# Gated DeltaNet stage: TensorE's order from a planner with four chains and a filler, instead of from the scheduler

## The chip, the cores and the metric

The kernel runs on one core of one Trainium2 chip. The metric is the device time of one execution in microseconds (us), as a median over runs. A core has five engines that work in parallel, each in the order of its own instruction stream: TensorE (PE; its weight loads are listed as PEld), VectorE (DVE), ScalarE (ACT), GpSimd (POOL) and SyncE (SP, which issues DMAs). An instruction that waits for another engine holds everything behind it on its own engine.

## The reference

Two DeepNorm layers over 512 positions of 1024 channels. Each layer is a token mixer, a LayerNorm, a squared-ReLU MLP and a LayerNorm. The mixer of the first layer, where the change lies, is a bidirectional gated DeltaNet with 8 heads of 128 key and 128 value channels:

```python
proj = jnp.matmul(h, w_in)
qkv = silu(_depthwise_conv(proj[..., :A_CONV_CH], conv_w))      # 5 taps, centred
z = proj[..., A_CONV_CH:A_CONV_CH + A_VW]
q = _l2norm(heads(q)) * (A_DK ** -0.5);  k = _l2norm(heads(k))
# per direction, in chunks: (I + A) sol = rhs, A strictly lower triangular; then
v_new = u_c - w_c @ state
o     = qd_c @ state + qk_c @ v_new
state = state * gl_c + kd_c.T @ v_new
o = _rmsnorm(o_f + o_b, norm_g) * silu(z);  out = o @ w_out
```

The second mixer (GLA) and the two MLPs are not touched.

## The kernel before

The function `gdn` keeps x transposed on chip (`xth`, `xtl`: a high and a low part) and treats the 8 heads as objects of `GdnHead`. The work of a head has five parts:

- **project**: four projections of the head, k, q, v and z (PSUM tiles `pjk`, `pjq`, `pjv`, `pjz`), 24 matmuls each: eight k-tiles by the three products of the helper `mm3` (L109, L110, L111). The weights come by DMA to `wst`, ACT casts the high part `wh` (L90) and DVE subtracts the low part `wl` (L91). k, q and v go through the 5-tap convolution `conv`: one multiply on ACT (L1032) and four scalar_tensor_tensor on DVE (L1036) into the tile `sil` of the head (four slots: k, q, v, z); z is copied (L1059). Then ACT loads the Silu table, applies Silu to the whole tile (L1065) and loads the exp/ln table back (L50).
- **rows**: four transposes of k, then four of q (L1082, PSUM tile `ktp`); for k a copy `kt` (L1085); for each four ACT squares with a sum (L1087). A chain of small DVE and ACT operations makes the normalisers and decays, which are split into three bf16 parts (`rsp`, 6 columns), transposed (L1112, `rtp`, 6 rows) and copied to `rt` (L1114).
- **solve**: inverts the triangular systems of both directions, 8 tiles of 128x128 at a time: kk, `ep` (L1147, `sel` times `rt`, a product over 6 rows), exponentials `E`, `ath`, three steps `hp` in blocks of 4, then five levels (4 to 64), each a `lv` product, a DVE or ACT step and two more `lv` products (L1220), then one correction (`nw`), `qk`, and the transposed v (`vt`).
- **recur**: four steps over the chunks, both directions side by side. Each step is a chain: product m1 on PE (L1312), `r` on DVE (L1314), product m2 (L1320), `vd` and `vn` on ACT (L1324, L1326), product m3 (L1332), `sn` on DVE or ACT (L1337, L1335), and again m1. Then 14 products make the output `op` (L1345).
- **finish**: RMSNorm of `op`, four transposes `otp` (L1368), times silu(z), split to `oh` and `ol` for the output projection.

After the heads, `out_pieces` makes the output projection of heads 0 to 5 (PSUM `oa`), and `out_last` adds x and heads 6 and 7 (`ob`), with LayerNorm and transposes.

The program order is a loop over heads: recur of head i-2, solve of i-1, project and rows of i, finish of i-2. The order on each engine is made by the framework's scheduler, which takes the earliest in program order that its own timing model has ready. The parts are generators that yield pairs of numbers, but the loop's `run` throws them away. The tile `sil` has three buffers: the project part of head h waits until head h-3 has let go of its tile. PSUM has three banks for projections, two for the solve (`ac`), two for recur and finish (`ch`) and **one** (`tp`) for kk, ktp, rtp and vt.

Of the kernel before, what the change touches and what calls it, by code (L numbers as in the profile page):

```python
# [17 lines left out]
P = 128  # L18
S = 512
D = 1024  # L20
KT = D // P
NT = S // P
# [779 lines left out]
A_H = 8  # L802
NEG = -1e30


class GdnConst:
# [36 lines left out]
    def masks(self):  # L843
        c, pool = self.c, self.pool
        G = c.nc.gpsimd
# [5 lines left out]
        sf = pool.tile([6, 2, P], F32, name="self", tag="E", bufs=2)  # L851
# [37 lines left out]
        n = P // 4  # L889
# [75 lines left out]
def gdn(c, w_in, conv_w, a_log, dt_bias, norm_g, w_out, ln_g, ln_b, x):  # L965
    tc, nc = c.tc, c.nc
    with c.banks(ch=2, pj=3, tp=1, ac=2), tc.tile_pool(name="gdn", bufs=1) as pool:
        last = load_x(c, x, ("ac", "ch", "tp"))
        g = GdnConst(c, pool, w_in, a_log, dt_bias, conv_w, norm_g, last)
        hi = [c.big.tile([P, 2, S], F32R, name=f"oh{t}", tag=f"xt{t}") for t in range(NT)]  # L970
        lo = [pool.tile([P, S], F32R, name="ol", tag="ol", bufs=A_H) for h in range(A_H)]
        heads = [GdnHead(c, pool, g, h, w_in, hi[h // 2][:, h % 2, :], lo[h]) for h in range(A_H)]
        lhs = lambda k, sl: (hi[k // 2][:, k % 2, sl], lo[k][:, sl])
        z = [[None, None] for t in range(NT)]
        early = list(range(6))

# [6 lines left out]
        def run(*gens):  # L983
            for gen in gens:
                for _ in gen:
                    pass

        done = set()
        for i in range(A_H + 2):
            old, mid, new = (heads[j] if 0 <= j < A_H else None for j in (i - 2, i - 1, i))  # L990
            if old:
                run(old.recur(done))
            if mid:
                run(mid.solve(done))
            if new:
                run(new.project(done), new.rows(done))
            if i >= A_H:
                load_z(i - A_H)
                run(c.out_pieces(w_out, early, lhs, z, "pj", (i - A_H,), 1))
            if old:  # L1000
                run(old.finish(done))
        par = c.load_ln(ln_g, ln_b, lambda j: pool.tile([P, S], F32, name="lnp", tag=("ath", "atl", "a4", "Xd")[j]))
        c.new_x()
        c.new_xt()
        c.out_last(w_out, [6, 7], lhs, z, ("ac", "pj"), par)


class GdnHead:
# [30 lines left out]
    def project(self, done):  # L1039

        c, pool, g, h = self.c, self.pool, self.g, self.h
        A = c.nc.scalar
        sil = pool.tile([P, 4, S], F32, name="sil", tag="sil", bufs=3)
        self.kq = kq = sil[:, 0:2, :]
        self.v, self.sz = sil[:, 2, :], sil[:, 3, :]
        for i, ci in enumerate((A_H + h, h, 2 * A_H + h, 3 * A_H + h)):
            if h == 0 and i == 0:
                ps = g.k0
            else:
                wh, wl = c.wcols(self.w_in, ci * P)  # L1050
                ps = c.bank([P, S], F32, name="pj" + "kqvz"[i], tag="pj")
                for k in range(KT):
                    c.mm3(ps, wh[:, k, :], wl[:, k, :], c.xth[:, k, :], c.xtl[:, k, :], k == 0, k == KT - 1)
                    if k < KT - 1:
                        yield 0.69, 0.0
            if i < 3:
                self.conv(sil[:, i, :], ps, ci)
            else:
                A.copy(self.sz, ps)  # L1059
            if i == 1 and h == 0:  # L1060
                c.exp_ln_after(A.activation(kq, kq, AF.Silu))
                done.add(("kq", h))
            elif i == 3:
                v = sil[:, 2 if h == 0 else 0:4, :]
                c.exp_ln_after(A.activation(v, v, AF.Silu))  # L1065
                done.add(("kq", h))
                done.add(("vz", h))
            yield 0.69, 0.0

    def rows(self, done):  # L1070
# [4 lines left out]
        yield 0.0, 6.0  # L1075
        kq = self.kq
        ssp = c.small.tile([P, 2, NT], F32, name="ssp", tag="ssp")
        junk = pool.tile([P, P], F32, name="junk", tag="junk", bufs=2)
        for i in range(2):
            ps = self.bank("ktp", tag="tp")  # L1080
            for n in range(NT):
                T.transpose(ps[:, n, :], kq[:, i, n * P:(n + 1) * P], c.ident)  # L1082
            if i == 0:
                self.kt = self.t2("kt", 3)
                A.copy(self.kt, ps)  # L1085
            for n in range(NT):
                A.activation(junk, ps[:, n, :], AF.Square, accum_out=ssp[:, i, n:n + 1])  # L1087
            yield 0.45, 4.0 if i == 0 else 6.5
# [14 lines left out]
        rs = c.small.tile([P, NT, 6], BF16, name="rsp", tag="rsp")  # L1103
# [7 lines left out]
        for n in range(NT):  # L1111
            T.transpose(rtp[:6, n, :], rs[:, n, :], g.idb)  # L1112
        self.rt = pool.tile([6, S], BF16, name="rt", tag="rt", bufs=2)
        A.copy(self.rt, rtp[:6, :, :].rearrange("p n i -> p (n i)"))  # L1114
# [13 lines left out]
        self.neg, self.kds = neg, kds  # L1128
        done.add(("rows", h))
        yield 0.25, 1.0  # L1130

    def solve(self, done):
# [9 lines left out]
        yield 0.9, 0.3  # L1142
# [10 lines left out]
        yield 0.63, 1.4  # L1153
# [18 lines left out]
        yield 0.45, 6.0  # L1172
# [3 lines left out]
        for it in range(3):  # L1176
# [6 lines left out]
            if it < 2:  # L1183
                yield 0.25, 0.7
# [4 lines left out]
        yield 0.25, 1.6  # L1189
# [35 lines left out]
        for s in (4, 8, 16, 32):  # L1225
# [10 lines left out]
            yield 0.7 if s == 4 else 0.25, 1.2  # L1236
# [4 lines left out]
            yield 0.5, 1.2  # L1241
# [5 lines left out]
        yield 0.25, 1.2  # L1247
# [6 lines left out]
        yield 0.5, 1.3  # L1254
# [13 lines left out]
        for n in range(NT):  # L1268
            T.matmul(qk[:, n, :], self.kc(n), self.qc(n), start=True, stop=True)
        if h:  # L1270
            yield 0.9, 0.0
            yield "op", h - 1
# [14 lines left out]
        yield "vz", h  # L1287
# [4 lines left out]
        A.copy(self.vt, ps)  # L1292
        done.add(("solve", h))
        yield 0.45, 1.0

    def recur(self, done):
# [4 lines left out]
        yield 0.0, 1.0  # L1301
        states, vns = [{}, {}], [{}, {}]
        cur = [None, None]
        for step in range(NT):
# [10 lines left out]
            if step:  # L1315
                yield 0.45, 0.6
# [11 lines left out]
            yield 0.45, 1.0  # L1328
            if step < NT - 1:
# [9 lines left out]
                yield 0.45, 0.6  # L1339
        self.op = op = self.bank("op", tag="ch")  # L1340
        for n in (1, 2, 0, 3):
# [4 lines left out]
            if n == 2:  # L1346
                yield 1.8, 0.0
        done.add(("op", h))

    def finish(self, done):  # L1350

        c, pool, g, op = self.c, self.pool, self.g, self.op
# [12 lines left out]
        yield 1.6, 6.0  # L1365
# [6 lines left out]
        V.tensor_tensor(self.olo, p, self.ohi.bitcast(F32), ALU.subtract)  # L1372
        done.add(("finish", self.h))
        yield 0.45, 0.0
# [39 lines left out]
```

## Time and profile before

| | |
|---|---|
| median of 3 runs | 1403.77 us (1403.65 to 1403.82) |
| span of the profiled execution | 1401.7 us (2.1 us less than the median) |
| Gated DeltaNet stage in that span | from 0 to about 437 us |
| PE busy | 1366.0 us, 97% of the span |
| DVE, ACT busy | 929.5 us (66%), 689.5 us (49%) |
| granted TensorE clock | 0.998 |

The page gives the busy time of each engine, the span in 40 slices, the chain that ended last and the costliest groups of instructions by line. A group's row has its count, its busy time and the mean duration of one. In the timeline each row has its start, its duration and its count. Matmuls overlap in their pipeline, so that their durations add up to more than the time they occupy; the distance between two starts tells what one occupies.

### The profile page before, as it was taken

The numbers are of one execution on the slowest core, as the hardware profiler recorded it, in microseconds if no ns is written. First come the engines' busy times: TensorE is split into PE (matmuls) and PEld (weight loads), VectorE is DVE, ScalarE is ACT, GpSimd is POOL, SyncE is SP. The second block draws the span as 40 slices with busy tenths as digits, with TensorE's granted clock in tenths as the row PEclk, the third lists the DMA queues.
The fourth block names the chain that finished last, engine by engine and source line by source line (L and its number), as shares of the span: only waits on it lengthen the run. The fifth ranks groups of instructions, "written<-read, shape, count | busy, mean of one in ns | idle before, by whom it ended". The sixth has DMA issues, their size and how long they took to land.

```text
span 1401.7 us, 20232 instructions
## 1 busy us (share of the span) xinstructions
PE 1366.0 (97%) x7933; PEld 1116.8 (80%) x7933; DVE 929.5 (66%) x1541; ACT 689.5 (49%) x1320; POOL 121.3 (9%) x168
## 2 busy tenths in 40 slices
PE   7999999999999999999999999999999999999997
PEld 6777777777777888888887888888878888888886
DVE  5787787778667365655556577877764655656655
ACT  3776657666633454444543354554433644445430
POOL 5000000000003300100000100000002000001000
PEclk9999999999999999999999999999999999999999
DMA  6212111211133964655431222222217666656121
GB/s 171 76 48 59 46 46 46 61 46 46 47 111 96 291 154 148 144 155 120 105 96 44 85 86 73 61 61 61 89 47 225 178 183 150 165 120 134 48 83 52
DMA packets 153030, 142.23 MB, mean 101 GB/s; under 512 B 8399, under 2 KB 123207, under 8 KB 152935
## 3 DMA queue, kind: packets, MB, share of 16 engines
q1 hardware_dynamic: 144112, 111.49, 26.5%
q0 software_dynamic: 8256, 29.37, 10.8%
q8 instruction: 62, 1.02, 0.3%
q14 instruction: 33, 0.27, 0.1%
q10 hardware_dynamic: 567, 0.08, 0.0%
HBM read 113.66 MB, written 2.10 MB: 83 GB/s over the span
## 4 chain that ended last, share of the span: by engine, by line
PE 59%; issue 23%; DMA 6%; ACT 6%; POOL 3%; DVE 2%; SPq 1%; DVEq 0%; POOLq 0%; ACTq 0%
DMA w2r<-w2r 4%; PE pj L109 3%; PE pj L111 3%; PE pj L110 3%; PE pjv L109 3%; PE pjv L111 3%; PE pjv L110 3%; PE scp L688 2%; DMA w2r<-in_mlp_w 2%; PE op L1345 2%; PE pjq L110 1%; PE pjq L111 1%; PE pjq L109 1%; PE op L776 1%; PE lv L1220 1%
## 5 line engine op out<-in xcount | busy, mean ns | idle before, releaser
L91 DVE TENSOR_TENSOR wl<-wst,wh 128x1024 fp32r<-128x1024 f32 x137 | 168.5, 1230 | 194.0 <-ACT wh L90 193.3
L90 ACT CAST wh<-wst 128x1024 fp32r<-128x1024 f32 x137 | 144.0, 1051 | 282.7 <-PE pj L110 170.2
L109 PE MATMUL pj<-xth,wh 128*128 128x512 f32 (+1 forms) x544 | 202.0, 372 | 1.7 <-ACT h L276 0.9
L111 PE MATMUL pj<-xth,wl 128*128 128x512 f32 (+1 forms) x544 | 201.7, 371 | 0.4 <-DVE wl L91 0.4
L110 PE MATMUL pj<-xtl,wh 128*128 128x512 f32 (+1 forms) x544 | 201.6, 371 | 0.4 <-DVE xtl L150 0.3
L91 DVE TENSOR_TENSOR w2l<-w2r,w2h 128x1024 fp32r<-128x1024 f32 x84 | 102.6, 1221 | 68.3 <-ACT w2h L90 68.3
L109 PEld LDWEIGHTS pj<-xth,wh 128*128 128x128 f32 x544 | 102.2, 188 | 20.4 <-ACT h L276 2.3
L110 PEld LDWEIGHTS pj<-xtl,wh 128*128 128x128 f32 x544 | 102.5, 188 | 18.6 <-DVE xtl L150 0.8
L111 PEld LDWEIGHTS pj<-xth,wl 128*128 128x128 f32 x544 | 102.4, 188 | 18.6 <-DVE wl L91 0.8
L90 ACT CAST w2h<-w2r 128x1024 fp32r<-128x1024 f32 x84 | 88.2, 1050 | 57.2 <-DMA w2r<-in_mlp_w 25.5
L303 POOL DMA_DIRECT2D w2r<-w2r x48 | 41.5, 902 | 398.2 <-DVE w2l L91 230.1
L90 ACT CAST ah<-h 128x1024 fp32r<-128x1024 f32 x40 | 42.1, 1054 | 42.1 <-PE pX L110 16.8
L110 PE MATMUL pX<-w2l,ah 128*128 128x512 f32 x144 | 56.1, 390 | 0.0
L109 PE MATMUL pX<-w2h,ah 128*128 128x512 f32 x144 | 56.1, 390 | 0.0
L111 PE MATMUL pX<-w2h,al 128*128 128x512 f32 x144 | 56.1, 390 | 0.0
L109 PE MATMUL pjv<-wh,xth 128*128 128x512 f32 x128 | 54.9, 429 | 0.0
L91 DVE TENSOR_TENSOR al<-h,ah 128x1024 fp32r<-128x1024 f32 x40 | 48.9, 1222 | 5.3 <-ACT ah L90 3.7
L160 ACT ACTIVATE rsy<-rsv 128x1 f32<-128x1 f32 (+1 forms) x28 | 5.6, 201 | 90.9 <-DVE rsv L159 90.9
L111 PE MATMUL pjv<-wh,xtl 128*128 128x512 f32 x128 | 50.2, 392 | 0.0
L110 PE MATMUL pjv<-wl,xth 128*128 128x512 f32 x128 | 49.9, 390 | 0.0
L1168 POOL TENSOR_TENSOR atl<-on,ath 128x512 f16<-128x512 f32 x16 | 20.9, 1306 | 323.4 <-ACT ath L1167 171.5
L109 PE MATMUL pjk<-xth,wh 128*128 128x512 f32 (+1 forms) x112 | 42.1, 376 | 0.5 <-ACT wh L90 0.5
(439 smaller groups left out, 3443.3 us busy)
## 6 DMA issues: line engine op xcount, KB each, us to landing
wst<-in_mlp_w SPq DMA_DIRECT2D x80, 512.0 KB, 4.0
w2r<-in_mlp_w SPq DMA_DIRECT2D x48, 512.0 KB, 4.3
w2r<-w2r POOLq DMA_DIRECT2D x48, 512.0 KB, 5.6
wst<-in_a_w_in SPq DMA_DIRECT2D x32, 512.0 KB, 4.0
wst<-in_b_w_in SPq DMA_DIRECT2D x32, 256.0 KB, 3.0
wst<-in_a_w_out SPq DMA_DIRECT2D x8, 512.0 KB, 3.8
wst<-in_b_w_in SPq DMA_DIRECT2D x8, 512.0 KB, 3.7
wst<-in_b_w_out SPq DMA_DIRECT2D x8, 512.0 KB, 3.6
```

The lines of the kernel that those rows point to most:

```text
L90: nc.scalar.copy(hi, src)
L91: nc.vector.tensor_tensor(lo, src, hi.bitcast(F32), ALU.subtract)
L109: mm(ps, ah, bh, start=start, stop=False, **kw)
L110: mm(ps, ah, bl, start=False, stop=False, **kw)
L111: mm(ps, al, bh, start=False, stop=stop, **kw)
L160: nc.scalar.activation(y, v, AF.Ln)
L303: nc.gpsimd.dma_start(blocks[a + (q,)], blocks[b + (q,)], accum_op=ALU.add)
L688: T.matmul(ps[:, n, :], kh[:, sl], qh[:, sl], start=True, stop=True)
L776: T.matmul(ops, l, r, start=i == 0, stop=i == len(mm) - 1)
L1168: G.tensor_tensor(atl[:, us, :], at, ath[:, us, :], ALU.subtract)
L1220: T.matmul(ps[:, u, :, :], lhs[:, u, :], cols(rhs, u, s, i), start=True, stop=True)
L1345: T.matmul(op[:, n, :], l, r, start=i == 0, stop=i == len(mm) - 1)
```

## The change

A class `Weave` decides the order on PE before the program is built. It walks over five generators: solve, recur, rows and finish, each over all heads one after the other, are the chains, in this order of preference; project, with the output projection of heads 0 to 5 behind it, is the filler. A generator yields either a pair (PE time of what it has just issued, time until its next step is ready) or the name of a mark that must have been set. At each turn the first chain that is ready by the planner's clock issues a step; if none is, the filler issues one (three matmuls, 0.69); if the filler is blocked too, the planner's clock moves on. `in_order` then ties PE's matmuls to that order. The orders of DVE, ACT and SP stay with the scheduler. The waiting times in the yields are new numbers. Head h may start its projections when `op` of head h-3 is issued, and finish of h-4.

z of a head is projected together with the next head: the order is z(h-1), k(h), q(h), v(h), and z(h-1) lies in the tile `sil` of head h. The last z stands alone. The tiles of the 6-row products (`sel`, `rsp`, `rt`) have 128 rows or columns, with zeros in the rest.

```diff
+class Weave:
+    def step(self, name, gen):
+        want = self.wants.get(name)
+        if want is not None and want not in self.done:
+            return "blocked"
+        self.wants[name] = None
+        if self.ready.get(name, 0.0) > self.t:
+            return "late"
+        got = next(gen, None)
+        if got is None:
+            return "over"
+        if isinstance(got[0], str):
+            self.wants[name] = got
+        else:
+            self.t += got[0]
+            self.ready[name] = self.t + got[1]
+        return "ran"
+    def run(self, chains, filler):
+        chains = dict(chains)
+        while chains or filler is not None:
+            for name in list(chains):
+                got = self.step(name, chains[name])
+                if got == "over":
+                    del chains[name]
+                if got in ("ran", "over"):
+                    break
+            else:
+                if filler is not None:
+                    got = self.step("filler", filler)
+                    if got == "over":
+                        filler = None
+                    if got in ("ran", "over"):
+                        continue
+                late = [self.ready[n] for n in chains if self.wants.get(n) is None and self.ready.get(n, 0.0) > self.t]
...
+                if late:
+                    self.t = min(late)
...
-        self.sel = pool.tile([6, 2, P], BF16, name="sel", bufs=1)
+        self.sel = pool.tile([P, 2, P], BF16, name="sel", bufs=1)
+        self.rs = pool.tile([P, NT, P], BF16, name="rsp", bufs=1)
+        G.memset(self.rs, 0.0)
...
-        for i in range(A_H + 2):
-            old, mid, new = (heads[j] if 0 <= j < A_H else None for j in (i - 2, i - 1, i))
-            if old:
-                run(old.recur(done))
-            if mid:
-                run(mid.solve(done))
-            if new:
-                run(new.project(done), new.rows(done))
-            if i >= A_H:
-                load_z(i - A_H)
-                run(c.out_pieces(w_out, early, lhs, z, "pj", (i - A_H,), 1))
-            if old:
-                run(old.finish(done))
+        def project():
+            todo = [(h, ci) for h in range(A_H) for ci in heads[h].weights()] + [(A_H, 4 * A_H - 1)]
...
+                if h < A_H and (i == 0 or todo[i - 1][0] != h):
+                    if h >= 3:
+                        yield "op", h - 3
+                    if h >= 4:
+                        yield "finish", h - 4
+                    heads[h].slots()
...
+                        if k < KT - 1:
+                            yield 0.69, 0.0
...
+                    elif kind == 2:
+                        t = head.sil if h else head.v
+                        if h:
+                            heads[h - 1].sz = head.sil[:, 3, :]
+                        c.exp_ln_after(A.activation(t, t, AF.Silu))
+                        done.add(("kq", h))
...
+            yield "finish", early[-1]
+            for hf in range(2):
+                yield "op", early[-1] + hf
+                load_z(hf)
+                yield from c.out_pieces(w_out, early, lhs, z, "pj", (hf,), 1)
...
+        def each(what):
+            for head in heads:
+                yield from getattr(head, what)(done)
+        with c.in_order(mybir.EngineType.PE):
+            Weave(done).run({w: each(w) for w in ("solve", "recur", "rows", "finish")}, project())
...
+    def weights(self):
+        out = [] if h == 0 else [3 * A_H + h - 1]
+        return out + [A_H + h, h, 2 * A_H + h]
...
         yield "kq", h
-        yield 0.0, 6.0
+        yield 0.0, 4.0 if h == 0 else 5.5
...
-            T.transpose(rtp[:6, n, :], rs[:, n, :], g.idb)
-        self.rt = pool.tile([6, S], BF16, name="rt", tag="rt", bufs=2)
+            T.transpose(rtp[:, n, :], rs[:, n, :], g.idb)
+        self.rt = pool.tile([P, S], BF16, name="rt", tag="rt", bufs=2)
...
-            yield 0.5, 1.2
+            yield 0.5, 1.4
...
-                yield 0.45, 0.6
+                yield 0.45, 1.3
```

In the changed kernel the transposes of rows stand at L1154, the convolution at L1123 and L1127, Silu at L1071, m1, m2, m3 at L1382, L1390, L1402, `op` at L1415 and `otp` at L1439.

**PE, between the last projection before Silu and the transposes of rows, in the middle heads.** The tiles m_… are the PSUM tiles of recur. Before, that last projection is pjz:

```order
L111 MATMUL pjz<-xth,wl 128x512
L109 MATMUL pjk<-xth,wh 128x512
L110 MATMUL pjk<-xtl,wh 128x512
L111 MATMUL pjk<-xth,wl 128x512
L1220 LDWEIGHTS ath
...
L110 MATMUL pjk<-xtl,wh 128x512
L1082 MATMUL ktp<-ident,sil 128x128
```

Between pjz and ktp stand 14 projection matmuls of the next head (pjk) and 24 `lv` products. With the change the last projection is pjv:

```order
L111 MATMUL pjv<-xth,wl 128x512
L1382 MATMUL m_2521<-sn,sil 128x128
L1382 MATMUL m_2525<-sn,sil 128x128
L1390 MATMUL m_2535<-r,xf 128x128
L1390 MATMUL m_2541<-r,xf 128x128
L1402 MATMUL m_2547<-vd,kt 128x128
L1402 MATMUL m_2551<-vd,kt 128x128
L1382 MATMUL m_2555<-sn,sil 128x128
L1382 MATMUL m_2559<-sn,sil 128x128
L1251 LDWEIGHTS a_2498
...
L1154 MATMUL ktp<-ident,sil 128x128 x4
```

Between pjv and ktp now stand eight products of recur and eight `hp` products, and no projection; the next projection matmul on PE comes only behind the 14 `op` products and `rtp`.

**ACT at the same place.** Before:

```order
L90 CAST wh<-wst 128x1024
L1059 COPY sil<-pjz 128x512
L1065 ACT_TABLE_LOAD
L1065 ACTIVATE sil<-sil 128x2048
L50 ACT_TABLE_LOAD
```

With the change:

```order
L1239 CAST ath<-on 128x512
L1123 ACTIVATE sil<-pjv,cw 128x512
L1394 ACTIVATE vd<-m_2535,kds 128x128
L1396 COPY vn<-m_2535 128x128
L1394 ACTIVATE vd<-m_2541,kds 128x128
L1396 COPY vn<-m_2541 128x128
L90 CAST wh<-wst 128x1024
L1071 ACT_TABLE_LOAD
L1071 ACTIVATE sil<-sil 128x2048
L50 ACT_TABLE_LOAD
L1157 COPY kt<-ktp 128x512
L1159 ACTIVATE junk,ssp<-ktp 128x128
```

What Silu waits for was a copy of pjz; it is now the whole convolution of pjv, which begins with the ACTIVATE of L1123 and goes on with four DVE instructions.

**PE at the end of the stage, from the last products of head 7 to its transposes.** Before:

```order
L1345 MATMUL op<-sn,qd 128x128
L109 MATMUL oa<-wh,oh_412 128x512
L110 MATMUL oa<-wl,oh_412 128x512
L111 MATMUL oa<-wh,ol 128x512
...
L1368 MATMUL otp<-ident,fo 128x128 x4
```

With the change:

```order
L1415 MATMUL op<-vn,qke 128x128 x2
L1415 MATMUL op<-sn,qd 128x128
L1439 MATMUL otp<-ident,fo 128x128 x4
L109 MATMUL ob<-wh,oh_416 128x512
L110 MATMUL ob<-wl,oh_416 128x512
```

The 12 `oa` and 11 `ob` matmuls that stood between `op` and `otp` have moved ahead of `op`.

More of the change, by code (lines that the diff above doesn't have):

```diff
@@ L1037, in conv, with slots @@
                                    ALU.mult, ALU.add)
[L1039 to L1068, printed above, removed]
+    def weights(self):
+        h = self.h
+        out = [] if h == 0 else [3 * A_H + h - 1]
+        return out + [A_H + h, h, 2 * A_H + h]
+    def slots(self):
+        self.sil = self.pool.tile([P, 4, S], F32, name="sil", tag="sil", bufs=3)
+        self.kq = self.sil[:, 0:2, :]
+        self.v = self.sil[:, 2, :]
     def rows(self, done):
@@ L1101, in rows @@
         V.tensor_tensor(rw, gc, rk, ALU.add)
-        rs = c.small.tile([P, NT, 6], BF16, name="rsp", tag="rsp")
+        rs = g.rs
         r1 = c.small.tile([P, NT, 2], F32, name="r1", tag="r1")
@@ L1111, in rows @@
         for n in range(NT):
-            T.transpose(rtp[:6, n, :], rs[:, n, :], g.idb)
-        self.rt = pool.tile([6, S], BF16, name="rt", tag="rt", bufs=2)
-        A.copy(self.rt, rtp[:6, :, :].rearrange("p n i -> p (n i)"))
+            T.transpose(rtp[:, n, :], rs[:, n, :], g.idb)
+        self.rt = pool.tile([P, S], BF16, name="rt", tag="rt", bufs=2)
+        A.copy(self.rt, rtp.rearrange("p n i -> p (n i)"))
         V.tensor_tensor(c0, rk, gc, ALU.subtract)
@@ L1364, in finish @@
         V.tensor_tensor(on, op, rs_.unsqueeze(2).to_broadcast([P, NT, P]), ALU.mult)
-        yield 1.6, 6.0
+        yield "vz", self.h
+        yield 0.0, 6.5
         otp = self.bank("otp", tag="ch")
```

75 lines of the change are left out of this document (51 added, 24 removed).

## The prediction

> **What bounds the kernel now.** I read the page's engine totals first, then PE's waits in the stage that changes, then PE's timeline, because the first two cannot both be taken at their word.
>
> ```profile
> PE 1366.0 (97%) x7933; PEld 1116.8 (80%) x7933; DVE 929.5 (66%) x1541; ACT 689.5 (49%) x1320; POOL 121.3 (9%) x168
> PE m L1320 <- DVE r L1314: 1.5, 3, 1.0
> PE hp L1179 <- DVE a L1171: 1.4, 3, 0.8
> 200.00:250.00 50.00, 49.31 (x415) 38.88 (x414) 40.02 (x86) 31.38 (x87) 2.32 (x2) 1.00 0.18 44
> 550.00:600.00 50.00, 50.00 (x221) 41.18 (x220) 30.32 (x31) 23.11 (x27) 6.88 (x8) 1.00 0.66 148
> ```
>
> PE looks full, and the two longest waits in the middle of the stage (60 to 440 us) come to 2.9 us in all. In the window rows (PE, PEld, DVE, ACT, POOL, clock, DMA) the DeltaNet stage has PE at 49.3 of 50 us, DVE at 40.0, ACT at 31.4; the MLP behind it has PE at 50.0. The Trainium skill, Perfetto Trace Analysis (Identifying the Most-Contended Engine), says that matmul busy time does not tell how near PE is to its limit and that the busy share of weight loads does. By that rule 38.9 against the MLP's 41.2 leaves some 5% of the stage to be won, which the trace's starts, below, bear out in kind.
>
> ```profile
> 210.91 0.39 PE L109 MATMUL pjk<-xth,wh 128*128 128x512 f32 x1
> 211.13 0.39 PE L110 MATMUL pjk<-xtl,wh 128*128 128x512 f32 x1
> 211.36 0.39 PE L111 MATMUL pjk<-xth,wl 128*128 128x512 f32 x1
> 211.59 0.41 PE L1220 MATMUL lv<-pz,Xd 128*128 128x64 f16 x8
> 211.83 0.40 PE L1220 MATMUL lv<-Xd,pz 128*128 128x64 f16 x8
> 212.06 0.47 PE L109 MATMUL pjk<-xth,wh 128*128 128x512 f32 x1
> 212.38 0.40 PE L110 MATMUL pjk<-xtl,wh 128*128 128x512 f32 x1
> 212.72 0.33 PE L1082 MATMUL ktp<-ident,sil 128*128 128x128 f32 x1
> 195.90 0.61 PE L1345 MATMUL op<-vn,qke 128*128 128x128 f32 x4
> 196.34 0.61 PE L1345 MATMUL op<-sn,qd 128*128 128x128 f32 x4
> 165.03 1.92 ACT L1065 ACTIVATE sil<-sil 128x2048 f32<-128x2048 f32 x1
> 301.44 1.92 ACT L1065 ACTIVATE sil<-sil 128x2048 f32<-128x2048 f32 x1
> ```
>
> A projection matmul shows 0.39 us but the next starts 0.23 us later; eight `lv` products take 0.24 us, four fp32 products of 128 columns 0.44 us. After a change from small products back to a projection, the first matmul takes 0.32 us, 0.085 more. The Silu of a head comes every 45.5 us (three heads in 136.4 us).
>
> What is PE's own part of that? A head has 96 projection matmuls (96 x 0.228 = 21.9), 100 fp32 products of 128 columns (100 x 0.111 = 11.1), 120 `lv` (3.6) and, counted at 0.03 to 0.23 us each, some 3.4 us of hp, nw, xp, ep and rtp: **40.0 us**. In the order before, a middle head has 26 runs of projections, 26 x 0.085 = **2.2 us**. The rest of the 45.5 us, **3.3 us**, are waits. So the whole that a better order can win is 5.5 us per head.
>
> **The change part by part.**
>
> *Fewer runs.* In the new order a middle head has 12 runs: 1.0 us, a gain of 1.2 us per head.
>
> *Waits.* A head now costs 40.0 + 1.0 + W; it breaks even at W = 4.5. W is not spread any more. The new order puts nine projection matmuls (2.0 us) between most links of solve; at this rate the filler runs ahead to its limit of three `sil` tiles and is then blocked until `op` of an older head. From pjv of a head to `rtp` PE has no projection left: a stretch of 10.2 us of matmul time (15.1 us once, at the third head) in which recur, hp and rows have only each other. In it stands ktp, 2.0 us of PE time behind pjv (eight products of two 0.111 us passes, and hp). What must happen in these 2.0 us:
>
> ```profile
> 200.47 0.39 PE L111 MATMUL pjv<-xth,wl 128*128 128x512 f32 x1
> 201.62 0.68 ACT L1032 ACTIVATE sil<-pjv,cw 128x512 f32<-128x512 f32 x1
> 202.90 0.74 DVE L1036 SCALAR_TENSOR_TENSOR sil<-pjv,cw,sil 128x510 f32<-128x510 f32 x1
> 207.26 0.74 DVE L1036 SCALAR_TENSOR_TENSOR sil<-pjv,cw,sil 128x510 f32<-128x510 f32 x1
> 208.86 0.58 ACT L1059 COPY sil<-pjz 128x512 f32<-128x512 f32 x1
> 209.46 1.28 ACT L1065 ACT_TABLE_LOAD   x1
> 210.75 1.92 ACT L1065 ACTIVATE sil<-sil 128x2048 f32<-128x2048 f32 x1
> 212.69 1.28 ACT L50 ACT_TABLE_LOAD   x1
> 215.08 0.59 ACT L1085 COPY kt<-ktp 128x512 f32<-128x512 f32 x1
> 215.56 0.28 ACT L1087 ACTIVATE junk<-ktp 128x128 f32<-128x128 f32 x1
> ```
>
> With empty queues: 0.7 + 4 x 0.74 + 1.92 = 5.6 us, and 0.2 to hand over, 5.8. In this trace the convolution of pjv ran from 200.7 to 208.0, 7.3 us, because other DVE work stood between its four instructions; with Silu 9.2. Here z's move counts: before, Silu waited for a copy of pjz, 0.58 us, and had 14 projection matmuls to hide in; now it waits for pjv's convolution and has none. So PE, in order, stands still at ktp for 3.8 us (empty queues) to 7.2 us. Behind ktp in PE's order wait m2, hp, m3 and all of solve. Then the one `tp` bank: the second ktp waits for the table load (1.28), the copy (0.5 to its successor) and four squares (0.25 each by their starts), 2.8 us, with `vd` and `vn` of recur now in between (0.8 more); 1.7 us of matmuls stand there, so 1.1 to 1.9 more. Last, `sn` stands on ACT behind eight `E` and one `ath`, and `Xd` behind the second four squares: about 1 us each. What W holds: from 3.8 (Silu alone, with the rest hidden in it) to 7.2 + 1.9 + 1 = 10.1. I take **9.0**, near the upper end, since the trace's convolution had the long latency. Then a middle head takes 50.0 us instead of 45.5: +4.5, four such heads, **+18**.
>
> The third head's stretch of 15.1 us has the same Silu wait and ten links of recur without filler, each a product, a DVE or ACT step and a hand-over: I take 14 us (bounds 5 and 16), 14 + 1.0 - 5.5 = **+9.5**. The last two heads have fewer rows to wait for (5 and 6 us): **+2**. The first two heads have filler everywhere: **-3** (bounds -4 and 0).
>
> *The end.* `otp` of head 7 now follows `op` at once.
>
> ```profile
> 413.99 0.39 PE L1345 MATMUL op<-sn,qd 128*128 128x128 f32 x2
> 420.69 0.69 DVE L1364 TENSOR_TENSOR fo<-op,ors 128x512 f32<-128x512 f32 x1
> 421.45 0.64 PE L1368 MATMUL otp<-ident,fo 128*128 128x128 f32 x4
> ```
>
> From the end of `op` to `otp` the finish chain took 7.2 us, covered by `oa` and `ob`. Uncovered it costs 5 to 7 us, and what follows needs `oh` of head 7, some 1.6 us more. The covering matmuls are not lost, they ran earlier. **+7** (bounds 3 and 8.5).
>
> *Padding.* The nearest rows are full products of the same kind:
>
> ```profile
> L1147 PE MATMUL ep<-rt,sel 6*128 6x512 bf16 x16 | 5.3, 381 | 0.0
> L1160 PE MATMUL ep<-mi,idb 128*128 128x512 bf16 x16 | 6.1, 383 | 0.0
> L1112 PE MATMUL rtp<-idb,rsp 128*6 128x128 bf16 x32 | 3.1, 219 | 0.1
> L1192 PE MATMUL xp<-idh,Dd 128*128 128x128 f16 x64 | 5.0, 220 | 0.0
> ```
>
> 381 against 383 ns, 219 against 220: nothing either way, and the copy `rt` has as many columns as before.
>
> *One more Silu* for the last z, with two table loads (2.6 us on ACT): it lies in a stretch with `oa` as filler; 0, at most 3.
>
> Sum: 18 + 9.5 + 2 - 3 + 7 = **+33.5 us**. The span becomes 1401.7 + 33.5 = 1435.2; the median lies 2.1 above the profiled span, so **1437 us**. With the lower bounds (4 heads x (3.8 + 1.0 - 5.5) = -2.8, third head +0.5, last two -2, first two -4, end +3) it is -5, 1398 us. With the upper ones (4 x 5.6 = 22, 11.5, 3, 0, 8.5) it is +45, 1449 us.
>
> **The rivals.**
>
> *The queues empty themselves (not slower).* While PE stands still, it gives DVE and ACT nothing new, so that the convolution runs near its 5.6 us and recur's links are paid inside the wait for Silu. This is the lower bound: 1398 us, faster by 0.4%. It decides if W stays under 4.5. For it: DVE has 20% of its time free, ACT 37%. Against it: in the stretch ACT's order puts pjv's first multiply behind eight `E` and two `ath`, and `a4` of 1.1 us stands on DVE before the first of the four.
>
> *The clock falls.*
>
> ```profile
> 6.10 4.21 PE L146 MATMUL tp<-ident,xt 128*128 128x128 f32 x20 [6.10 <-POOL blk L876]
> 11.20 1.50 PE L146 MATMUL tp<-ident,xt 128*128 128x128 f32 x12 [0.90 <-DMA xt<-in_x]
> ```
>
> After 6.1 us without work 20 transposes took 0.21 us each, and some 5 us later 12 took 0.125. If each wait for Silu brought PE back to that pace, 2 us would be lost per stretch, in six stretches 12 us: 1449 us. For it, the waits last 3 to 7 us; against it, the page grants the full clock in all slices but for this start. The Trainium skill, TensorE: Matmul & The Clock Gate (What's actually happening), lets the clock drop to half after an idle window of about 3.4 us; by that rule the waits at ktp would be long enough in some heads.
>
> *The change doesn't do what it says.* The order as built has the new sequence, and the only thing left would be that another engine's order undoes it; then the time would stay near 1404.
>
> **How the numbers follow.** Forecast (waits in the dry stretch outweigh the gains) 0.69, clock 0.10, empty queues 0.19, no effect 0.02. Differences under 0.2% can't be told from none here. Empty queues and the first heads' gains end faster with 0.15, same with 0.04; with the last rival, faster 0.15, same 0.05, slower 0.80. The likeliest case's own range is 1416 to 1455; the range for 8 in 10 goes from the lower bound, 1398, to the upper one with the cold clock, 45 + 12 = 57, 1461.
>
> **What would show it.** Right: PE idle before ktp in the waits, put down to ACT's Silu, 3 us or more in each of heads 2 to 6; Silu every 50 us; fewer PE busy us than span by far more than now; projections in runs of nine; an idle PE of 5 us or more at the last otp, with DVE's `fo` as the releaser; ep and rtp at 381 and 219 ns still. Wrong: Silu every 44 us or less, or a convolution of pjv under 6 us from its last matmul. A granted clock under 1.0 in the stage would show the second rival.

## The result and the profile after

The changed kernel took **1505.9 us** (median of 4 runs, 1503.1 to 1512.7) against 1403.7 us for the kernel before: a ratio of 1.0731, 95% interval 1.0714 to 1.0748. It is slower, as forecast, but by 102 us where 33.5 were forecast, and far outside the range. Its profiled execution has a span of 1502.1 us, 100.4 more than before.

From its page, the busy time of the engines:

```profile
PE 1392.6 (93%) x7932; PEld 1152.7 (77%) x7933; DVE 938.7 (62%) x1541; ACT 698.1 (46%) x1323; POOL 119.1 (8%) x169
```

The waits of PE in the stage (0 to 545 us), and windows of 50 us in it (PE, PEld, DVE, ACT, POOL, clock, DMA share, GB/s):

```profile
PE ktp L1154 <- ACT sil L1071: 28.0, 7, 7.0
PE m L1402 <- ACT vn L1396: 10.8, 11, 3.7
PE otp L1439 <- DVE fo L1434: 4.4, 1, 4.4
200.00:250.00 50.00, 41.54 (x327) 33.49 (x326) 33.36 (x66) 26.57 (x71) 2.27 (x2) 0.92 0.17 43
250.00:300.00 50.00, 43.04 (x350) 35.09 (x349) 36.03 (x75) 26.01 (x70) 2.27 (x2) 0.91 0.14 34
```

No wait in the stage of the kernel before reached 2 us once its first product had run; now PE stands 28.0 us for the Silu, as foretold, all engines do less in the same time, and the clock is below 1.0 in the middle of the stage.

**Where the 100 us are.** The first output product `op` of heads 0, 5 and 7 in the timelines, before and then after:

```profile
110.66 0.50 PE L1345 MATMUL op<-vn,qke 128*128 128x128 f32 x3
332.88 0.49 PE L1345 MATMUL op<-vn,qke 128*128 128x128 f32 x2
410.99 0.49 PE L1345 MATMUL op<-vn,qke 128*128 128x128 f32 x2
```

```profile
140.18 0.56 PE L1415 MATMUL op<-vn,qke 128*128 128x128 f32 x1
423.87 0.57 PE L1415 MATMUL op<-vn,qke 128*128 128x128 f32 x3
510.17 0.49 PE L1415 MATMUL op<-vn,qke 128*128 128x128 f32 x2
```

| stretch of the stage | before | after | more |
|---|---|---|---|
| up to the first `op` | 110.7 | 140.2 | 29.5 |
| five heads, `op` of head 0 to 5 | 222.2 (44.4 each) | 283.7 (56.7 each) | 61.5 |
| the last two heads | 78.1 | 86.3 | 8.2 |
| from the `op` of head 7 to the end of the span | 990.7 | 991.9 | 1.2 |

**One middle head.** Solve of a head begins with kk, has its exponentials and `hp` up to `xp`, then its five levels up to `nw`, then its last products; solve of the next head begins behind it. The timelines give these four points, before and after:

```profile
228.83 0.28 PE L1141 MATMUL kk<-sil 128*128 128x128 f32 x1
248.74 0.23 PE L1192 MATMUL xp<-idh,Dd 128*128 128x128 f16 x1
265.34 0.22 PE L1262 MATMUL nw<-Dd,ath 128*128 128x128 f16 x1
273.65 0.28 PE L1141 MATMUL kk<-sil 128*128 128x128 f32 x1
```

```profile
228.10 0.27 PE L1213 MATMUL kk<-sil 128*128 128x128 f32 x1
251.06 0.53 PE L1264 MATMUL xp<-idh,Dd 128*128 128x128 f16 x3
275.51 0.23 PE L1334 MATMUL nw<-Dd,ath 128*128 128x128 f16 x1
283.50 0.27 PE L1213 MATMUL kk<-sil 128*128 128x128 f32 x1
```

kk to `xp` took 19.9 us and takes 23.0; `xp` to `nw` 16.6 and 24.4; `nw` to the next kk 8.3 and 8.0. So 7.8 of the 10.6 us that this head lost lie in the levels, where PE hardly stood still: up to 257.9 us the products of recur stand in the links, and from there on projections, nine in most links. The part from kk to `xp`, which the prediction looked at, lost 3.1.

The stretch without projections begins between kk and `xp`. The last projection matmul of one and the first of the next, from the timeline, are 24.6 us apart; the third line is the last projection before the next such stretch:

```profile
289.39 0.40 PE L111 MATMUL pjv<-xth,wl 128*128 128x512 f32 x1
313.96 0.47 PE L109 MATMUL pjz<-xth,wh 128*128 128x512 f32 x1
345.48 0.40 PE L111 MATMUL pjv<-xth,wl 128*128 128x512 f32 x1
```

The chain of waits around its first half, in order of time:

```profile
288.03 1.65 ACT E L1235 x7
290.66 0.50 PE m L1382 x2
291.19 0.61 DVE r L1384 x2
291.80 1.54 DVE a L1243
293.34 0.66 DVE sil L1127
...
296.08 0.67 DVE sil L1127
296.82 1.28 ACT L1071
298.11 1.91 ACT sil L1071
300.04 1.28 ACT L50
...
303.85 0.80 PE m L1402 x2
```

Between 288 and 304 us the chain is on ACT and DVE but for one product of half a microsecond: exponentials, `r` and `a4`, the four steps of v's convolution, Silu between its two table loads, and behind it the copy and squares of k. The recurrence's own `vd` and `vn` stand in the same ACT queue behind the Silu, so that the third product (L1402) waits there too. The second half is PE's own: from 303.85 us to the next projection it does not wait again, and until 309.9 us it works at half clock:

```profile
303.85:309.90 6.05, 6.05 (x55) 5.89 (x56) 3.46 (x10) 3.12 (x12) 0.00 (x0) 0.50 0.00 0
```

### The profile page after: what moved, and what is told of

Read it like the earlier page. It is cut to its first block, busy times and chain, and to the rows that moved or that the text cites. A ratio compares the mean times of both kernels' runs of the same rounds, so it can differ in the third digit from the quotient of the medians.

```text
span 1502.1 us, 20213 instructions
## 1 busy us (share of the span) xinstructions
PE 1392.6 (93%) x7932; PEld 1152.7 (77%) x7933; DVE 938.7 (62%) x1541; ACT 698.1 (46%) x1323; POOL 119.1 (8%) x169
## 4 chain that ended last, share of the span: by engine, by line
PE 59%; issue 19%; DVE 6%; ACT 6%; DMA 5%; POOL 2%; DVEq 0%; POOLq 0%; ACTq 0%; SPq 0%
PE pj L110 4%; PE pj L109 4%; PE pj L111 4%; DMA w2r<-w2r 4%; PE pjv L109 3%; PE pjv L111 3%; PE pjv L110 3%; PE scp L688 2%; PE lv L1292 2%; PE op L1415 2%; PE pjk L109 1%; PE pjk L111 1%; PE pjk L110 1%; PE pjq L109 1%; PE oa L109 1%
## 5 line engine op out<-in xcount | busy, mean ns | idle before, releaser
L1240 POOL TENSOR_TENSOR atl<-on,ath 128x512 f16<-128x512 f32 x16 | 19.2, 1219 | 408.1 <-ACT ath L1239 408.1
```

The costliest lines, as they stand in the source:

```text
L1240: G.tensor_tensor(atl[:, us, :], at, ath[:, us, :], ALU.subtract)
```

## The experiments

Times are medians of 4 to 10 runs for e1 to e5, e11 and e12, and single runs for the others. The kernel before, run beside them, took 1403.8 to 1404.5 us (one run beside e9 and e10 took 1407.9). The edits are shown in part where "..." stands. "A head" is the mean of the five heads between `op` of head 0 and of head 5.

**The change's parts by themselves, in the scheduler's order.** Padding alone (e1):

```diff
-        self.sel = pool.tile([6, 2, P], BF16, name="sel", bufs=1)
+        self.sel = pool.tile([P, 2, P], BF16, name="sel", bufs=1)
...
-            T.transpose(rtp[:6, n, :], rs[:, n, :], g.idb)
+            T.transpose(rtp[:, n, :], rs[:, n, :], g.idb)
...
```

> The kernel before with the padding alone: the row tile, its four transposes, the copy of their result and the selector at 128 rows in place of 6. Padding free (the prediction's step): 1403 to 1406 us. Rival, that the larger transposes and copy lie on the path of every head: 0.5 us by eight heads, 1407 to 1408.

z with the next head's projections (e2):

```diff
-        for i, ci in enumerate((A_H + h, h, 2 * A_H + h, 3 * A_H + h)):
+        for i, ci in enumerate((A_H + h, h, 2 * A_H + h, 3 * A_H + h - 1)[:4 if h else 3]):
...
```

> The kernel before, loops and scheduler kept, with z of head h-1 projected ahead of k, q and v of head h, so that the Silu waits for the convolution of v instead of the copy of z; z of head 7 alone in the ninth turn. Theory that the loss sits in the written order (filler spent early, then a stretch without any): within 10 us of before, since the scheduler puts other work under the convolution. Rival, that the moved z is the loss by itself: 5.5 us of cover gone from under the convolution in seven heads, so 1430 to 1442. Rival, a shorter tail makes it faster: 1398.

e1 took 1401.2 us, ratio 0.9985 (0.9975 to 0.9994); e2 1402.6 us, 0.9991 (0.9981 to 1.000). Neither is the loss, and e1 is a little below its range of 1403 to 1406. Both together (e12):

> The kernel before, with the scheduler's order kept, and the two other parts of the change made together: padding (ratio 0.9985 by itself) and z with the next head's (0.9991 by itself). If the two gains add: 1399 to 1402, faster than both kernels by about 0.2 percent. If one stands for the other: 1402 to 1404.

1399.0 us, ratio 0.9961 (0.9948 to 0.9975): **0.4% below the kernel before**, and so faster than both kernels. The two gains by themselves would give 0.9976, so that they about add. In the profiles most of the gain lies ahead of the first `op`, which starts at 105.4 us in place of 110.7.

So the loss comes with the written order. Three tries at what in it.

**The Silu's wait (e5):** z last in the filler, so that the Silu no longer trails v's convolution.

```diff
-        out = [] if h == 0 else [3 * A_H + h - 1]
-        return out + [A_H + h, h, 2 * A_H + h]
+        out = [] if h == 0 else [3 * A_H + h - 1]
+        return [A_H + h, h, 2 * A_H + h] + out
```

> The changed kernel with one edit: within a head's filler z of the head before comes last, behind k, q and v, so that the Silu waits for one copy of z and the convolution of v runs under the 5.5 us of z's matmuls. Theory that the Silu's wait for the convolution of v is most of the loss: the 28.0 us that PE waited for the Silu at the transpose of k nearly vanish and the time falls to 1470 to 1480. Theory that the stretch without projections is long because the whole chain of dependent steps of solve and recurrence runs there, at the pace of VectorE and ScalarE, and the Silu is only where PE happens to stand: the wait moves to other rows and the time is 1495 to 1506.

1498.5 us (1.0672, 1.0646 to 1.0698). The wait for the Silu left the list of e5's waits altogether, and others took its place:

```profile
PE m L1402 <- ACT vn L1396: 34.5, 15, 5.5
PE rtp L1184 <- DVE rsp L1181: 12.2, 4, 4.6
```

A head went from 56.7 to 55.1 us. PE had been standing at ktp because PE's order put ktp there; the stretch is nearly as long without that wait, 23.2 us in three middle heads in place of 23.9 to 24.6. The second theory's range holds.

**The clock (e4):** matmuls of no use where the plan has nothing ready.

```diff
...
                 if late:
-                    self.t = min(late)
+                    if min(late) - self.t >= 0.45:
+                        self.bank = warm(self.bank)
+                        self.t += 0.45
+                    else:
+                        self.t = min(late)
...
```

> The changed kernel with one projection-sized matmul of no use (its result is never read) put into the order for each 0.45 us in which the plan has nothing ready, some 13 us of matmuls in each stretch without projections, 97 us over the stage; the waits for the other engines stay. What it tells is the clock's share: of the changed kernel's matmuls in the half-clock spells of the stage, those that follow one another without a wait take 27 us more than the same at full clock. Theory that the clock falls because of the waits and adds its own 27 us: granted clock 1.0 in the stage and 1470 to 1485. Rival, that the clock is most of the loss: 1420 to 1450. Rival, that the added matmuls delay the links they stand between, or that the clock still falls: 1510 to 1560.

1507.3 us. The whole stage in the changed kernel and in e4:

```profile
0.00:545.00 545.00, 453.81 (x3418) 372.31 (x3420) 349.11 (x736) 272.21 (x721) 44.69 (x71) 0.89 0.20 54
0.00:545.00 545.00, 470.96 (x3554) 381.13 (x3555) 346.15 (x729) 270.40 (x718) 44.47 (x71) 0.93 0.20 54
```

The mean clock rose from 0.89 to 0.93, and the time did not fall. But the run does not take the low clock away, as the first theory asked, and the matmuls it adds may cost what it gains. The clock's own share stays open. An estimate for the stretch shown above: of the 6.05 us that PE works there without a wait at clock 0.50, full clock would take half, about 3 us of 24.

**Fewer matmuls per link (e3):**

```diff
-            yield 0.7 if s == 4 else 0.25, 1.8 if s in (4, 32) else 1.4
+            yield 0.7 if s == 4 else 0.25, 1.2
-            yield 0.5, 1.4
+            yield 0.5, 1.2
...
```

> The changed kernel with the planned latencies of the solve lowered to near the ones that stood in the code before (1.2 for 1.4 and 1.8, 0.7 for 1.3, 6.0 for 7.5, none after the key-query product): six projection matmuls between two links instead of nine, so the projections last longer, and the work between the last projection of one head and the first of the next shrinks from 10.2 us of matmuls to 4 to 6 in the middle heads. Theory of the spent filler: the time falls by a third to a half of what the change cost, to 1450 to 1475, and the clock recovers with it. Rival, that the moved z is the loss (the Silu still waits for v): 1495 to 1510. Rival, that nine were needed to cover a link: slower than the changed kernel, 1515 to 1530.

1501.4 us (1.0696, 1.0680 to 1.0712): no third of the loss came back. The number lies in the range given to the moved z, which e2 and e5 speak against. The Silu's wait fell to 17.1 us, but this plan put other steps too early, such as the last products of the solve:

```profile
PE nw L1356 <- DVE qke L1348: 10.9, 8, 2.1
```

**What sets the pace.** VectorE first (e6, three of four shifted taps left out):

```diff
-        for k in (0, 1, 3, 4):
+        for k in (0,):
```

> The changed kernel with three of the four shifted taps of each convolution left out (the output is then not the reference's): VectorE has 9 passes of 0.66 us less for each head, 6 us, of which those of v lie in the stretch without projections, between the recurrence's own VectorE steps. Theory that VectorE and ScalarE set the length of that stretch: 3 to 5 us less a head, 1470 to 1480. Theory that PE's half clock and its matmuls set it: 1495 to 1506. Theory that only the wait for the Silu counts: as much as v's three taps, 2 us a head, 1490.

1481.2 us: 24.7 less. The start gained 12.9 of it, a head 2.1: in the middle it was no more than v's three taps. That is the size the third theory gave, though its reason, that only the wait for the Silu counts, does not fit e5; the first theory's 3 to 5 us a head did not come.

Seven of eight k steps left out of the projections, in the changed kernel (e7) and in the one before (e8):

```diff
-                    for k in range(KT):
-                        c.mm3(ps, wh[:, k, :], wl[:, k, :], c.xth[:, k, :], c.xtl[:, k, :], k == 0, k == KT - 1)
+                    for k in range(1):
+                        c.mm3(ps, wh[:, k, :], wl[:, k, :], c.xth[:, k, :], c.xtl[:, k, :], True, True)
```

> The changed kernel with one of the eight k steps of each projection (the output is then not the reference's): 31 projections lose 21 matmuls of 0.227 us, 148 us of PE time in the stage, and the filler for the links is nearly gone. Theory that PE's matmuls plus waits in the stretch make the period: most of the 148 us is saved, 1360 to 1400. Theory that a chain of dependent steps makes the period, with PE's matmuls beside it: 1470 to 1505.

> The same cut in the kernel before. If PE's matmuls bound it, as its 90 percent of busy time in the stage suggests, most of the 148 us is saved: 1260 to 1300. If the chain of solve, one head after another, was as long as PE's work, it stays: 1370 to 1400.

1517.4 and 1408.7 us: 148 us of PE work gone, and neither kernel faster; both lie above all the ranges named. But these runs have a second cause, seen in windows of e7 and of e8:

```profile
250.00:300.00 50.00, 26.43 (x210) 21.39 (x209) 31.20 (x65) 27.21 (x77) 2.27 (x2) 0.69 0.16 43
```

```profile
250.00:300.00 50.00, 37.55 (x364) 30.70 (x364) 42.35 (x89) 34.73 (x101) 2.32 (x2) 0.79 0.22 64
```

Without these projections the clock falls to 0.69 and 0.79 here, and in e8 DVE becomes the fullest engine, 42.35 of 50 us. So e8 decides nothing for the kernel before. (Its expectation put PE at 90 percent there; the windows of the kernel before have 97 to 99 from 50 to 400 us.) e7 shows that the changed kernel with hardly any filler is not bound by PE's work: PE is busy 26.4 of 50 us, and the rest is waiting on other engines. How long its chain of steps would be at full clock, and so whether that chain bound the changed kernel, e7 does not tell, as its small products ran at the lower clock too.

One level (s = 4) of the solve left out: two links of the chain, 0.7 us of PE work a head.

```diff
-        for s in (4, 8, 16, 32):
+        for s in (8, 16, 32):
```

> The changed kernel without the level s = 4 of the solve in each head (the output is then not the reference's): 24 products of 0.029 us, 0.7 us of PE's own work a head, but two links of the chain, each with its VectorE step and with nine projection matmuls beside it. Theory that the solve of one head after another sets the period, and nine matmuls in a link that needs less lengthen it: two links of 2.5 us, 4 to 5 us a head, 1466 to 1475. Theory that PE's matmuls plus the waits of the stretch without projections set it, the links with filler being dense: 0.7 us a head, and the filler that is not spent there shortens the stretch no further than that, 1495 to 1505.

> The same level left out of the kernel before. If the chain of the solve sets its period too: two links of 1.5 to 1.8 us, 3 to 3.6 us a head, 1375 to 1381. If PE's matmuls set it: 0.7 us a head, 1397 to 1400.

The changed kernel (e9) went to 1474.6 us, 31 less, a head from 56.7 to 52.8. The kernel before (e10) went to 1400.2 us, 3.6 below its usual time (7.7 below the one run beside it), a head from 44.4 to 43.6. The first theory's range holds for e9; e10 lies at the end of the second's. `op` of heads 0 and 5, e9 and e10:

```profile
131.20 0.56 PE L1415 MATMUL op<-vn,qke 128*128 128x128 f32 x1
395.13 0.61 PE L1415 MATMUL op<-vn,qke 128*128 128x128 f32 x2
```

```profile
108.92 0.49 PE L1345 MATMUL op<-vn,qke 128*128 128x128 f32 x3
326.70 0.50 PE L1345 MATMUL op<-vn,qke 128*128 128x128 f32 x3
```

This tells the two kernels apart: a link of the solve is worth 2 us a head after the change and about 0.4 before it, where the 0.8 us for two links is hardly more than the 0.7 us of PE work that went with them. With the written order the chain of the solve, one head behind the other, sets the pace; before, PE's work fits better. Each is a single run. And a level left out also leaves the projections beside it for later, so that e9 does not separate a shorter chain from a filler that lasts longer.

**The order kept, its plan changed (e11).**

```diff
-                        yield "op", h - 3
+                        yield "k", h - 3
...
-                        c.mm3(ps, wh[:, k, :], wl[:, k, :], c.xth[:, k, :], c.xtl[:, k, :], k == 0, k == KT - 1)
-                        if k < KT - 1:
-                            yield 0.69, 0.0
+                        for j, (l, r) in enumerate(((wh, c.xth), (wh, c.xtl), (wl, c.xth))):
+                            nc.tensor.matmul(ps, l[:, k, :], r[:, k, :], start=k + j == 0, stop=k == KT - 1 and j == 2)
+                            if k < KT - 1 or j < 2:
+                                yield 0.23, 0.0
...
-        yield 0.0, 4.0 if h == 0 else 5.5
+        yield 0.0, 4.0 if h == 0 else 12.4
...
-            yield 0.7 if s == 4 else 0.25, 1.8 if s in (4, 32) else 1.4
+            yield 0.7 if s == 4 else 0.25, {4: 1.4, 32: 1.4}.get(s, 1.0)
...
```

> The changed kernel, its four chains and its order of z, k, q, v kept, with the plan alone changed: the filler is given out matmul by matmul (0.23 us) and not in threes, the planned latencies of the solve's links are 1.0 to 1.4 in place of 1.4 to 2.2, the transposes of k and q of the next head are planned 12.4 us behind its convolution and not 5.5, and the projections of head h wait for the last key product of head h-3, a link before its output. The filler then lasts to within a few us of the next head's, so that no stretch is without it, and a link is no longer than it needs. Theory that links lengthened by nine matmuls and the stretch without any are the loss of the middle heads: they come back to about 45 us and the clock to 0.99, 1435 to 1455 (start and end of the stage stay as in the changed kernel). Theory that the written order of four chains is itself the loss (each wait on PE holds up all chains): 1480 to 1506.

1446.9 us, ratio 1.0301 (1.0284 to 1.0317): 59 of the 102 us came back, within the first theory's range. A window, and `op` of heads 0, 5 and 7:

```profile
200.00:250.00 50.00, 46.93 (x396) 37.59 (x396) 39.11 (x85) 32.45 (x94) 2.96 (x2) 1.00 0.17 43
127.19 0.47 PE L1418 MATMUL op<-vn,qke 128*128 128x128 f32 x2
363.15 0.49 PE L1418 MATMUL op<-vn,qke 128*128 128x128 f32 x2
452.38 0.49 PE L1418 MATMUL op<-vn,qke 128*128 128x128 f32 x2
```

A head takes 47.2 us (about 45 were expected), the clock is 1.00, and DVE's busy time is back at 39 of 50 us. What remains against the kernel before is 16.5 us up to the first `op`, 13.7 in the five heads and 11.1 in the last two, where no projections are left to give out.

Which of the edits did it? Four were taken back out of e11, each by itself. A fifth, longer planned waits in finish (8.0 and 3.2 us for 6.5 and 2.5), stayed in all of them:

> The spread plan with the changed kernel's latencies of solve and recurrence put back (1.4 to 2.2, 7.5 behind the exponentials). If links longer than they need are the loss: ten links of the levels at about 0.6 us more, 6 us a head, 1475 to 1500. If the stretch or the rows are: 1447 to 1455.

> The spread plan with the transposes of the next head's k and q planned 5.5, 4.0 and 6.0 us apart again, in place of 12.4, 2.7 and 7.0. If PE standing at them for the Silu is a loss of its own: 3 to 5 us a head, 1470 to 1490. If other work stands there anyway: 1447 to 1455.

> The spread plan with the projections of head h held until the whole output of head h-3 stands in the order, a link later than in the spread plan. If a stretch without projections costs more than its own length: 1460 to 1485. If a stretch of a few us is harmless: 1447 to 1455.

> The spread plan with the filler given out in threes of 0.69 us again, so that a link of 1.2 us gets six matmuls, 1.36 us. If the grain matters by itself: 0.2 us a link, some 2 to 4 us a head, 1460 to 1475. If not: 1447 to 1455.

| taken back out of e11 | us (one run) | against e11 | a head |
|---|---|---|---|
| e13: planned waits of solve and recur | 1475.5 | +28.6 | 50.4 |
| e14: later ktp | 1462.6 | +15.7 | 50.3 |
| e15: earlier release of the projections | 1481.5 | +34.6 | 51.3 |
| e16: filler in single matmuls | 1463.1 | +16.2 | 50.0 |

All four lose, and the losses add up to 95 us where all of them together won 59: the edits depend on each other. That fits e3 and e5, which changed one thing in the changed kernel and won 4.5 and 7 us. Only e14 ended outside both ranges named for it.

The traces show two kinds of loss. In e13, e15 and e16 the middle heads have stretches without projections again, of 7.4 to 10.5, 17.1 to 18.2 and 8.0 to 9.5 us; in e11 none is longer than 5.1 there. In e15 three of the five heads end in such a stretch and took 53.1, 56.6 and 55.1 us; the two others took 44.0 and 47.7. In e14 none is longer than 5.7 us there. Instead PE stands at ktp for the Silu, 8.8 us in 4 waits from 184 to 386 us, and at `rtp` for 3.7 us in 4, together 3.1 us a head, which is what a head lost against e11; in e11's list of waits for its middle heads neither stands. So with the filler given out evenly the wait for the Silu does cost its length.

## Why the prediction was right or wrong

- **"Waits", a middle head 40.0 + 1.0 + W, W = 9.0.** Direction right, size wrong. A head took 56.7 us, so W was 15.7. The step that failed is the price of the stretch without projections: 10.2 us of matmuls and 9.0 of waits, 19.2 us. The stretch shown took 24.3 us, the 24.6 above less the matmul itself. PE in it, and in the third head's stretch:

```profile
289.62:313.96 24.34, 17.69 (x153) 15.76 (x153) 14.30 (x42) 15.29 (x46) 2.27 (x2) 0.65 0.09 23
104.09:144.80 40.71, 26.39 (x193) 23.04 (x193) 20.83 (x50) 19.86 (x57) 2.27 (x2) 0.66 0.06 15
```

  The waits were not too low: PE was idle for 6.7 us and, in the third head, 14.3, where 9.0 and 14 were forecast, and the Silu's wait was there at 28.0 us in 7 waits, 4.0 each, within its bounds of 3.8 to 7.2. Too low was PE's own time, 17.7 us for 10.2 and 26.4 for 15.1. The sum took each product at the pitch it has in a dense row at full clock. In the stretch the products stand in small groups that depend on each other (four of recur show 0.71 us, where the sum has 0.44), and the clock stood at 0.65. (Busy is by the profile, where the ends of matmuls are modelled.) The rest of the head was right: 40.0 + 1.0 - 10.2 = 30.8 us forecast, 31.5 from 313.96 to 345.48. Along the chain of the solve the same loss shows as longer links in that rest (16.6 to 24.4 us from `xp` to `nw`): they used up filler that was missing later. The prediction named this ("the filler runs ahead") but counted it as neutral; e11 and e15 show that it is not. The base was a little long, too: 45.5 us came from three heads, and five by `op` give 44.4, so that W = 3.4 would have broken even.
- **"The first two heads have filler everywhere: -3", the third +9.5.** Together +6.5, measured +29.5 up to the first `op`. Here the words were right and the sign wrong: filler everywhere is what lengthened the first solve. Its `xp` and `nw`, before and then after:

```profile
76.05 0.45 PE L1192 MATMUL xp<-idh,Dd 128*128 128x128 f16 x5
91.80 0.22 PE L1262 MATMUL nw<-Dd,ath 128*128 128x128 f16 x1
```

```profile
75.05 0.34 PE L1264 MATMUL xp<-idh,Dd 128*128 128x128 f16 x3
104.10 0.23 PE L1334 MATMUL nw<-Dd,ath 128*128 128x128 f16 x1
```

  15.7 us became 29.1 while PE was full of later heads' projections, which were then missing from 103.9 to 144.8 us, the third head's stretch above, where 15.1 + 14 us were forecast.
- **"The last two heads +2", "the end +7".** The last head lost 6.9 us, the one before it 1.3, and the rest of the span 1.2: 9.4 against 9 forecast. The 23 `oa` and `ob` matmuls now ahead of `op` are some 5.3 us of it (an estimate at 0.23 us each), which leaves 2.9 for the two heads and 6.5 for the end, both near the forecast. The releaser at the last `otp` is `fo`, as said, at 4.4 us where 5 or more were named.
- **"Padding 0".** It held in e1, where the padded rtp and ep take 221 and 379 ns against 219 and 381; e1's small gain was not foreseen, and its cause was not looked for. In the changed kernel rtp shows 219 ns as its median, and the padded ep 413 on average.
- **The rivals.** "Queues empty themselves" fell: ACT and DVE were emptier (26 and 33 to 36 of 50 us, against 31 and 40), yet the chain ran through them one step after another. "The clock falls" came true beside the forecast: it stood at half for 17.1 us in the stretch shown below, which by the estimate above cost about 3 us where 2 per stretch were named. By the Trainium skill, TensorE: Matmul & The Clock Gate (What's actually happening), the clock drops after an idle window of about 3.4 us; here it dropped at 292.8 us with no wait over 0.9 us ahead of it. The clock's own share of the loss stays open, since e4 did not restore it and in e11 it came back together with the order.
- **What would show it.** Projections in runs of nine and the Silu's wait were as said, and the convolution of pjv did not end within 6 us of its last matmul (289.6 to 296.8 us); the heads came every 56.7 us and not every 50.

## What to carry to other kernels

When work without dependences is given out between the links of a chain, give each link what its wait needs and no more: a matmul too many lengthens the chain at once and is missing at its end. A stretch of dependent small products takes longer than their pitch in a dense row: price it by their shown durations and by the clock it will get. To know whether a chain or PE sets the pace, take a link out of the chain (two links were worth 3.9 us a head in one kernel and 0.8 in the other, at nearly the same PE work). A wait in the list tells where PE stands, and not what its removal will win: e5 removed the longest wait in the list, 28 us, and won 7.

## What the runs showed of the hardware that was not expected

The clock fell to half without a long wait of PE ahead of it. Windows of the changed kernel around one such spell, and PE's timeline just ahead of it:

```profile
286.00:292.80 6.80, 5.35 (x28) 3.77 (x26) 4.92 (x9) 5.54 (x21) 2.27 (x2) 1.00 0.22 65
292.80:309.90 17.10, 11.90 (x89) 10.54 (x90) 9.18 (x22) 11.28 (x31) 0.00 (x0) 0.50 0.12 31
```

```profile
290.66 0.71 PE L1382 MATMUL m<-sn,sil 128*128 128x128 f32 x4 [0.88 <-ACT sn L1405]
291.60 0.75 PE L1390 MATMUL m<-r,xf 128*128 128x128 f32 x4 [0.22 <-DVE r L1384]
```

No wait ahead of 292.8 us was longer than 0.9 us; what had ended at 289.6 were the projections, and the small products that follow keep PE partly busy only. With projections given out evenly (e11) the clock is 1.00 in every window of 50 us from 150 to 350 us; with seven eighths of them left out it is 0.69 and 0.79 in the windows of e7 and e8. So in these runs the clock was high where projections stood close together. Whether the lower clock is why e8 won nothing back, or the fuller DVE, is not shown.
